# Identity products in TensorE's gaps: a planner thread that issues matrix products nobody reads

## The chip, the cores and the metric

One core of one Trainium2 chip. The metric is the device time of one execution in microseconds, lower is better. TensorE is called PE in the profile, VectorE DVE, ScalarE ACT, GpSimd POOL; SP is the engine that issues most DMAs.

## The reference, cut to what matters

Two transformer blocks, one after the other, on one sequence of 256 tokens with 1024 features in float32. Each has an adaptive modulation computed from a vector `c`, a mixer and a gated feed-forward layer of width 2816.

```python
# first block: attention and mLSTM side by side
merged = sigmoid(g_a) * (y_a @ w_branch_attn) + sigmoid(g_m) * (y_m @ w_branch_mlstm)
x = x + gate_m * rms_norm(merged @ w_out, g_post_mix)
h2 = modulate(rms_norm(x, g_pre_ffn), shift_f, scale_f)
ff = (silu(h2 @ w_ffn_gate) * (h2 @ w_ffn_up)) @ w_ffn_down
x = x + gate_f * rms_norm(ff, g_post_ffn)
# second block: gMLP and RWKV-7 side by side
x = layer_norm(x, emb_ln_g, emb_ln_b)
p = (x * (1 + sc1) + sh1) @ w_in
mix = concat([gmlp(p[..., :2*MIX_A]), rwkv7(p[..., 2*MIX_A:])]) @ w_out_2
x = layer_norm(ALPHA * x + gt1 * mix)
f = (silu(gu[..., :FFN]) * gu[..., FFN:]) @ w_ffn_out      # gu = (x * (1+sc2) + sh2) @ w_ffn_in
x = layer_norm(ALPHA * x + gt2 * f)
```

## The kernel before, in words

All large products use float32 operands split in two (`hi` and `lo` parts in a reduced type): a product is three passes, hi by hi, lo by hi, hi by lo. A weight arrives by a DMA of 512 KB into a `raw` buffer, ACT rounds it to `whi`, DVE subtracts to `wlo`, and then PE uses it. `xhi`, `xlo` and `wx` are the same thing in other buffers.

The first mixer is written out in program order, and the framework below the kernel orders its instructions. It does not have to keep program order between instructions that don't depend on each other: where the kernel wants an early one held back it says so (`issue_after` in `main`).

From the output projection of the first mixer on, a planner orders the work (`planned`, L1259, and class `Plan`). It keeps a clock of its own, a cost for each instruction (`cost`, L279) and a set of threads, which are generators that issue instructions and yield. What `Plan` emits keeps its emission order on PE, DVE, ACT and POOL. The order is fixed when the kernel is built: the chip knows nothing of the planner's clock, and an instruction without a dependency starts as soon as its engine reaches it.

Threads have ranks. Chains that follow each other step by step (norms, residuals, the RWKV recurrences) have ranks 0 to 8. The stream of weights and their products has rank 9 (`FILL`); a modulation product on PE, `ada` (L1097), has rank 10 where it is used. `turn` (L128) first steps any ready thread of rank below 9. Then it takes the ready thread of the lowest rank from 9 on, `th`. If PE is idle in the plan and `low` holds, `th` is stepped at once and what it issues has rank -1 (`boost`), ahead of all else that waits for PE:

```python
        low = idle and (self.tick(self.now) or self.warm(self.now) < WARM)
        if th and th.pe == 0 and low:
            self.step(th, True)
            return True
```

Only after that does `choose` (L152) give each engine the ready instruction of lowest rank. `warm` (L169) sums the columns of the products that ended in the last `TICK` (3.4133 us) of the planner's clock, and `WARM` is 4800 columns. A full float32 product of 128 x 128 counts 4 x 128 = 512 columns and is planned at 0.2153 us; a small product of the recurrences, in a part of the array, counts far fewer for its time.

The stream is not ready while it waits for an event ("f1.0": the first half of the next layer's input; "ya", "base0", "yb0", "yb1": results of the second mixer) or has 24 products waiting (`AHEAD`). The planned stages are: `mix1` (down projection, 215 to 237 us), `f1` and `ffn1` (to 438), `m2` (second mixer, to about 605), `mix2` (to 626), `f2` and `ffn2` (to 821), and the last norm.

PSUM tiles: `mm` has 4 buffers, `sm` 3 (`pssm`, L441), `ad` 1. The planner tracks which of them are free (`tile`, `ready`, `release`). `drop` marks a tile as no longer needed.

Of the kernel before, what the change touches and what calls it, by code (L numbers as in the profile page):

```python
# [18 lines left out]
P = 128  # L19
# [32 lines left out]
WARM = 4800.0  # L52
# [336 lines left out]
class Builder:  # L389
# [436 lines left out]
    def stream(self, jobs):  # L826
# [17 lines left out]
        while queue or nxt[0]:  # L844
# [8 lines left out]
            for y in emit(sl):  # L853
                fill()
                yield y

    @staticmethod
    def cut(sl, k, cols):

        o = k * cols % 512  # L860
        return [t[:, o:o + cols] for t in sl[0][k * cols // 512]]
# [397 lines left out]
    def planned(self, mT, close):  # L1259

        nc, io, tc = self.nc, self.io, self.tc
        fl = self.plan = Pool.plan = Plan()
        self.nc = TimedCore(fl, nc)
        self.hT, self.hid, self.acc, self.gb = {"m1": mT}, {}, {}, {}
        w1, w2 = io["w_ada"][0], io["w_ada_2"][0]
        cv1, cv2 = self.cv
        c2 = self.c2
        self.free = ["w", "w", "w"]
        self.set_phase("m1", "t2", "t2", "t2")
        fl.at["gate.mix1"] = fl.at["aff.f1"] = 0.0  # L1270
        fl.add(9, self.stream(self.weights()))

        def out(name):
            def get():
                if name not in self.hT:
                    self.hT[name] = self.new_hT(name)
                return self.hT[name]
            return get
        for b in range(NB):
            fl.add(0, self.chain_rms("mix1", b, out("f1"), "f1"), "mix1.%d0" % b)  # L1280
        fl.run("mix1.end")
        close()
        fl.drop(*mT)
        with tc.tile_pool(name="ffn1", bufs=1) as pool:
            self.open_ffn(pool, "f1")
            jobs = self.ada_gate(w1, cv1, 5, io["b_ada"], "ffn1", io["g_post_ffn"][0])
            jobs += self.ada_affine(w2, cv2, 0, c2["b1"][:, 0:8], 1, c2["b1"][:, 8:16], c2["emb_g"], c2["emb_b"], "m2")
            fl.add(8, self.ada(jobs))
            fl.add(7, self.rows2(io["emb_ln_g_2"], io["emb_ln_b_2"], "emb"), "gate.ffn1")
            fl.add(7, self.mixer2_consts(), "gate.ffn1")  # L1290
            for b in range(NB):
                fl.add(0, self.chain_ln("ffn1", b, self.rms_residual, out("m2"), "m2", lambda: self.gb["emb"]), "ffn1.%d0" % b)
            fl.add(10, self.ada(self.ada_affine(w2, cv2, 3, c2["b2"][:, 0:8], 4, c2["b2"][:, 8:16], c2["ln1_g"],
                                               c2["ln1_b"], "f2"), True), "ffn1.00")
            fl.run("ffn1.end")
            fl.drop(*self.hT["f1"])
        with tc.tile_pool(name="mix2", bufs=1) as pool:
            self.ph = Pool(pool, h=32, PP=1)
            self.hT["y2"] = None
            self.set_phase("m2", "hT")  # L1300
            self.mixer2()
            for b in range(NB):
                fl.add(0, self.chain_ln("mix2", b, self.alpha_residual, out("f2"), "f2", lambda: self.gb["ln1"]), "mix2.%d0" % b)
            fl.run("mix2.end")
            fl.drop(*self.hT["y2"])
        with tc.tile_pool(name="ffn2", bufs=1) as pool:
            self.open_ffn(pool, "f2")
            fl.add(8, self.gate(w2, cv2, 5, io["b_ada_2"], "ffn2"), "f2.x")
            fl.add(7, self.rows2(io["ln2_g_2"][0], io["ln2_b_2"][0], "ln2"), "f2.x")
            for b in range(NB):  # L1310
                fl.add(0, self.chain_ln("ffn2", b, self.alpha_residual, None, "out", lambda: self.gb["ln2"]), "ffn2.%d0" % b)
            fl.run("out.1")
# [1118 lines left out]
```

## Time and profile before

| | |
|---|---|
| median of 3 runs | 835.97 us (831.27 to 840.24) |
| the profiled execution | 835.19 us |
| its span, first to last instruction | 833.4 us |
| PE busy | 779.9 us, 94% |
| DVE busy | 582.2 us, 70% |
| ACT busy | 380.2 us, 46% |
| mean granted PE clock | 0.978 |

Rows below are from the profiled execution. A time in a row counts from the span's start. In rows of a timeline the first number is the start, the second the duration to the last end, then engine, line, operation, written tile <- read tiles, shapes and count; in brackets stands how long the engine had been idle and who released it. Line 376 is the planner's own call, so all planned instructions have it. The granted clock 1.00 is 2.4 GHz and 0.50 is 1.2 GHz; values between are means over a stretch that has both.

### The profile page before, as it was taken

The page shows a single profiled execution, that of the slowest core. Times are in us where ns is not written, and L with a number is a line of the kernel's source. Part 1 is how long each engine was busy: PE and PEld are TensorE (multiplying, and loading weights), DVE is VectorE, ACT ScalarE, POOL GpSimd, SP SyncE. Part 2 cuts the span into 40 slices and gives each one's busy share as a digit, 9 for nine tenths or more (in the row PEclk, how much of TensorE's full clock was granted, in tenths as well). Part 3 has the DMA queues.
Part 4 walks back from the last instruction along what each step waited for, and adds up shares of the span by engine and source line. Part 5 has one row for each costly group of instructions (what it writes and reads, how often), then busy time and mean ns, then how long its engine had stood idle before and what let it go on. Part 6 is the DMA issues. An engine that isn't in the chain of part 4 may idle for free.

```text
span 833.4 us, 14964 instructions
## 1 busy us (share of the span) xinstructions
PE 779.9 (94%) x5912; PEld 670.4 (80%) x5912; DVE 582.2 (70%) x1036; ACT 380.2 (46%) x599; POOL 61.7 (7%) x143
## 2 busy tenths in 40 slices
PE   4999899999989999999998999998896999999994
PEld 4778467999867999998885878886675899999883
DVE  3458766886778977876456467997559778666446
ACT  3346854454555444445425574443235444445330
POOL 3014010100020310000002011001001000000000
PEclk9999999999989999999999999999998999999997
DMA  9986489796759899997559617687445689766611
GB/s 268 319 265 178 168 289 275 215 254 179 246 157 316 259 308 261 306 311 242 186 162 265 177 51 182 171 250 207 149 126 164 183 256 300 213 201 216 212 52 51
DMA packets 205078, 178.94 MB, mean 215 GB/s; under 512 B 24052, under 2 KB 171712, under 8 KB 205008
## 3 DMA queue, kind: packets, MB, share of 16 engines
q1 hardware_dynamic: 201456, 168.37, 69.2%
q0 software_dynamic: 3552, 9.63, 3.6%
q8 instruction: 46, 0.75, 0.4%
q14 instruction: 24, 0.20, 0.1%
HBM read 175.06 MB, written 2.90 MB: 214 GB/s over the span
## 4 chain that ended last, share of the span: by engine, by line
PE 79%; DVE 11%; DMA 2%; ACT 2%; issue 2%; POOL 2%; SPq 1%; POOLq 0%; DVEq 0%; ACTq 0%
PE mm L376 53%; PE sm L376 5%; PE mm L434 4%; PE mm L435 4%; PE mm L436 4%; DVE x L376 2%; PE ad L554 1%; DVE wlo L376 1%; DVE wlo L427 1%; POOL hr_r L376 1%; DMA ada_raw<-in_w_ada_dram 1%; PE ad L376 1%; DMA raw<-in_w_in_dram 1%; SPq L376 1%; ACT whi L376 1%
## 5 line engine op out<-in xcount | busy, mean ns | idle before, releaser
L376 DVE TENSOR_TENSOR wlo<-raw,whi 128x1024 fp32r<-128x1024 f32 (+1 forms) x135 | 163.7, 1216 | 99.8 <-ACT whi L376 98.9
L376 ACT CAST whi<-raw 128x1024 fp32r<-128x1024 f32 (+1 forms) x135 | 140.7, 1045 | 187.5 <-PE mm L376 153.0
L376 PE MATMUL mm<-f_hi,wlo 128*128 128x256 f32 x560 | 156.7, 280 | 0.0
L376 PE MATMUL mm<-f_lo,whi 128*128 128x256 f32 x560 | 156.4, 279 | 0.0
L376 PE MATMUL mm<-f_hi,whi 128*128 128x256 f32 x560 | 156.0, 279 | 0.0
L376 PEld LDWEIGHTS mm<-f_lo,whi 128*128 128x128 f32 x560 | 105.8, 189 | 0.3 <-issue 0.2
L376 PEld LDWEIGHTS mm<-f_hi,whi 128*128 128x128 f32 x560 | 105.5, 188 | 0.6 <-issue 0.5
L376 PEld LDWEIGHTS mm<-f_hi,wlo 128*128 128x128 f32 x560 | 105.2, 188 | 0.7 <-issue 0.7
L427 DVE TENSOR_TENSOR wlo<-raw,whi 128x1024 fp32r<-128x1024 f32 x42 | 51.2, 1220 | 23.3 <-ACT whi L426 23.3
L426 ACT CAST whi<-raw 128x1024 fp32r<-128x1024 f32 x42 | 44.1, 1049 | 44.2 <-DMA raw<-in_w_in_dram 19.9
L434 PE MATMUL mm<-h_hi,whi 128*128 128x256 f32 (+1 forms) x184 | 52.9, 287 | 0.8 <-ACT qkv L1383 0.8
L436 PE MATMUL mm<-h_hi,wlo 128*128 128x256 f32 (+1 forms) x184 | 51.6, 280 | 0.0
L435 PE MATMUL mm<-h_lo,whi 128*128 128x256 f32 (+1 forms) x184 | 51.5, 280 | 0.0
L376 PE MATMUL mm<-m_hi,wlo 128*128 128x256 f32 (+1 forms) x152 | 42.8, 287 | 0.2
L376 PE MATMUL mm<-m_hi,whi 128*128 128x256 f32 (+1 forms) x152 | 42.4, 283 | 0.3 <-DVE kT L376 0.3
L376 PE MATMUL mm<-m_lo,whi 128*128 128x256 f32 (+1 forms) x152 | 42.3, 281 | 0.0
L434 PEld LDWEIGHTS mm<-h_hi,whi 128*128 128x128 f32 (+1 forms) x184 | 34.3, 187 | 3.1 <-ACT qkv L1383 1.7
L435 PEld LDWEIGHTS mm<-h_lo,whi 128*128 128x128 f32 (+1 forms) x184 | 34.2, 186 | 0.5 <-issue 0.5
L436 PEld LDWEIGHTS mm<-h_hi,wlo 128*128 128x128 f32 (+1 forms) x184 | 34.3, 187 | 0.0
L376 DVE SCALAR_TENSOR_TENSOR part<-ada_raw,cs,part 128x512 f32<-128x512 f32 x42 | 31.4, 746 | 0.6
L376 PE MATMUL mm<-wlo,hid_hi 128*128 128x512 f32 x80 | 31.3, 391 | 0.0
L376 PE MATMUL mm<-whi,hid_hi 128*128 128x512 f32 x80 | 31.2, 390 | 0.0
(546 smaller groups left out, 1775.3 us busy)
## 6 DMA issues: line engine op xcount, KB each, us to landing
ada_raw<-in_w_ada_dram SPq DMA_DIRECT2D x96, 512.0 KB, 5.9
raw<-in_w_in_dram SPq DMA_DIRECT2D x60, 512.0 KB, 5.5
raw<-in_w_ffn_in_dram SPq DMA_DIRECT2D x44, 512.0 KB, 5.1
raw<-in_w_ffn_gate_dram SPq DMA_DIRECT2D x22, 512.0 KB, 5.8
raw<-in_w_ffn_up_dram SPq DMA_DIRECT2D x22, 512.0 KB, 5.9
raw<-in_w_ffn_down_dram SPq DMA_DIRECT2D x22, 512.0 KB, 5.1
raw<-in_w_ffn_out_dram SPq DMA_DIRECT2D x22, 512.0 KB, 3.6
raw<-in_w_out_dram SPq DMA_DIRECT2D x16, 512.0 KB, 4.2
```

What stands on the lines that cost most here:

```text
L376: return lambda *args, **kw: self.plan.issue(self.name, op, args, kw, lambda: f(*args, **kw))
L426: self.nc.scalar.copy(hi, raw)
L427: self.nc.vector.tensor_tensor(lo, raw, hi.bitcast(F32), op=ALU.subtract)
L434: mm(out, lhsT=l[0], rhs=r[0], start=start, stop=False)
L435: mm(out, lhsT=l[0], rhs=r[1], start=False, stop=False)
L436: mm(out, lhsT=l[1], rhs=r[0], start=False, stop=stop)
L554: nc.tensor.matmul(ps[32 * g:32 * g + 32, :], lhsT=cv["rep"][:, 2 * (s - 1) + g, :], rhs=raws[s - 1 + g // 2][:, g % 2, :], start=s == 1, ...
```

## The change

A new thread of rank 30 is added when the planned part begins, and lives until the event "out.1", the end of the kernel. Whenever it is stepped while PE is free in the plan and `warm` is under `WARM`, it takes an `sm` tile, issues two float32 products of the identity with itself into its first 128 columns, drops the tile and yields until both have ended in the plan; otherwise it asks again 0.2 us later. Nothing reads the tile.

```diff
+    def keep_warm(self, until):
+
+        fl = self.plan
+        while until not in fl.at:
+            if fl.free["tensor"] <= fl.now and fl.warm(fl.now) < WARM:
+                ps = self.pssm("warm")
+                for _ in range(2):
+                    self.nc.tensor.matmul(ps[:, 0:P], lhsT=self.ident, rhs=self.ident, start=True, stop=True)
+                fl.drop(ps)
+                yield
+            else:
+                yield 0.2
+
...
         fl.add(9, self.stream(self.weights()))
+        fl.add(30, self.keep_warm("out.1"))
```

## Rows read from the trace of the kernel before

**Rows 1.** Page: granted PE clock in 40 slices of 20.8 us, in tenths.

```profile
PEclk9999999999989999999999999999998999999997
```

**Rows 2.** Stretches of 20 us: length, busy PE, PEld, DVE, ACT, POOL, then clock, DMA.

```profile
240.00:260.00 20.00, 16.65 (x62) 12.19 (x63) 17.79 (x34) 11.65 (x23) 4.02 (x6) 0.83 0.82 260
...
440.00:460.00 20.00, 16.96 (x111) 11.55 (x103) 13.27 (x25) 9.57 (x17) 3.65 (x4) 0.91 0.99 281
...
620.00:640.00 20.00, 14.28 (x62) 11.58 (x61) 18.88 (x37) 10.43 (x20) 2.43 (x4) 0.83 0.49 144
```

**Rows 3.** Stretches of 4 us, same columns, after the first and second gap.

```profile
244.00:248.00 4.00, 3.84 (x12) 2.64 (x11) 3.54 (x8) 0.00 (x0) 2.31 (x3) 0.52 0.56 177
...
448.00:452.00 4.00, 3.38 (x16) 2.41 (x20) 2.57 (x7) 1.90 (x5) 1.23 (x2) 0.66 1.14 326
```

**Rows 4.** Timeline of PE, 237 to 252 us: the first gap.

```profile
237.55 1.09 PE L376 MATMUL sm<-ident,xn 128*128 128x128 f32 x8
242.05 0.79 PE L376 MATMUL mm<-whi,f_hi 128*128 128x512 f32 x1 [3.40 <-ACT f_hi L376]
...
247.26 1.36 PE L376 MATMUL sm<-ident,xn 128*128 128x128 f32 x8 [0.16 <-DVE xn L376]
...
252.06 0.50 PE L376 MATMUL mm<-xlo,f_hi 128*128 128x512 f32 x1 [0.31 <-DVE xlo L376]
```

**Rows 5.** Stretches cut at the stages' own bounds, columns as in rows 2.

```profile
215.00:237.00 22.00, 22.00 (x97) 17.75 (x96) 15.21 (x25) 11.38 (x22) 1.51 (x3) 1.00 0.61 194
...
242.00:252.00 10.00, 8.71 (x27) 5.69 (x27) 8.43 (x19) 5.20 (x13) 2.93 (x4) 0.71 0.70 216
556.00:573.00 17.00, 13.93 (x246) 10.61 (x244) 16.34 (x43) 6.64 (x12) 1.80 (x3) 1.00 0.76 214
573.00:600.00 27.00, 24.57 (x393) 17.66 (x393) 16.08 (x33) 8.99 (x18) 2.73 (x3) 1.00 0.62 199
...
621.00:642.00 21.00, 14.66 (x62) 11.26 (x61) 20.36 (x40) 11.14 (x20) 2.43 (x4) 0.84 0.51 148
821.50:833.40 11.90, 0.06 (x1) 0.00 (x0) 7.68 (x15) 0.00 (x0) 0.54 (x1) 0.64 0.18 66
```

**Rows 6.** Timeline of PE in `m2`: full float32 products and what starts after them.

```profile
572.27 0.71 PE L376 MATMUL mm<-wsT,vv 128*128 128x128 f32 x4 [1.42 <-DVE vv L376]
573.07 0.45 PE L376 MATMUL sm<-G,M 64*64 64x64 f32 x8
...
585.69 1.16 PE L376 MATMUL mm<-wsT,vv 128*128 128x128 f32 x8
586.78 0.62 PE L376 MATMUL ad<-ada_raw,cs 128*32 128x256 f32 x2
```

**Rows 7.** Groups of PE by form, 556 to 600 us: count, busy, mean ns, idle before.

```profile
L376 PE MATMUL ad<-ada_raw,cs 128*32 128x256 f32 x80 | 6.8, 389 | 0.0
...
L376 PE MATMUL mm<-wsT,vv 128*128 128x128 f32 x16 | 2.8, 300 | 1.4 <-DVE vv L376 1.4
L376 PE MATMUL sm<-RB,W 128*64 128x64 f32 x64 | 2.8, 227 | 0.9 <-DVE F L376 0.9
```

**Rows 8.** Chain that ended last, shares by line: 572 to 604, 621 to 643, 0 to 14 us.

```profile
by line: PE sm L376 48.6%; PE mm L376 12.2%; PE ad L376 7.1%; PE adr L376 6.9%; POOL hr_r L376 5.2%; issue 4.1%; DVE gl_t L376 4.0%; DVE y L376 2.2%; DVE mix L376 2.2%; ACT rx L376 2.0%; ACT Pm L376 1.9%; ACT part L376 1.9%; ACT XT L376 1.2
...
by line: DVE x L376 24.3%; DVE wlo L376 15.4%; DVE res L376 11.2%; DVE ln_st L376 10.9%; DVE hf L376 10.6%; DVE f_lo L376 8.8%; PE mm L376 8.7%; issue 6.8%; DVE xlo L376 3.1%; DVE ln_mv L376 1.1%; DVE ln_ve L376 0.6%; DVEq L376 0.1%
...
by line: DMA ada_raw<-in_w_ada_dram 59.8%; PE sm L742 9.0%; PE ad L752 7.7%; SPq L512 5.2%; issue 3.3%; SPq L749 3.1%; SPq L629 2.5%; POOL ident L616 2.1%; POOL ident L615 1.5%; POOL vrows L510 1.1%; POOL mhalf L619 0.3%; POOLq L2420 0.1%
```

**Rows 9.** Timeline where the planned part begins, and one early POOL instruction.

```profile
10.20 1.12 POOL L1328 MEMSET invf<- 128x1 f32 x32
...
209.67 1.05 ACT L376 CAST whi<-raw 128x1024 fp32r<-128x1024 f32 x1 [1.46 <-issue]
...
215.16 0.86 PE L376 MATMUL mm<-whi,merged_hi 128*128 128x512 f32 x3
...
218.68 0.42 ACT L1672 ACTIVATE merged_hi<-mg 128x256 fp32r<-128x256 f32 x1 [1.30 <-DVE mg L1671]
```

## The prediction

> **What bounds the kernel now.** The page first: PE is busy for 94% of the span, and its granted clock has two dips ahead of the last slice [rows 1]; a third, shallower, shows only in shorter stretches. I cut the planned part into stretches of 20 us. Three of them are below full clock: 0.83, 0.91 and 0.83 [rows 2]. They are the three hand-overs from one layer to the next, where PE waits for a norm. Between them, in the big layers, PE is the bound and at 2.4 GHz: 215 to 237 us has 22.00 busy of 22.00 at clock 1.00 [rows 5].
>
> So there are two questions: what the lost clock costs on the path that sets the end, and what the new products cost where they land.
>
> The first hand-over shows how to answer the first. PE does the transposes for the first half of the tokens at 237.55, then stands for 3.40 us until ACT has made `f_hi`, and resumes at 242.05 [rows 4]. From 244 to 248 the clock is 0.52, which is 1.2 GHz nearly throughout [rows 3]; over 242 to 252 the mean is 0.71, so 2.9 us of full clock are missing [rows 5]. But PE then waits again: the next transposes (247.26) for DVE's `xn`, the product at 252.06 for DVE's `xlo` [rows 4]. What PE lost, it mostly lost inside a wait.
>
> The third hand-over is clearer. Of the chain between 621 and 643 us PE has 8.7%, nearly all of the rest are DVE's links, and DVE is busy 20.36 of 21.00 us [rows 8, 5].
>
> **The change part by part.** It removes nothing. It adds pairs of identity products wherever the planner, by its own clock, finds PE idle, fewer than 4800 columns in its look-back and no ready stream or `ada` thread. On the chip a pair has no input to wait for, so it runs as soon as PE reaches it: it is free where the next real product would have waited anyway, and costs its full time where not.
>
> *Price of a pair.* No identity product is in the trace. The nearest is `wsT` by `vv`, also full float32, 128 x 128; the trace keeps two records per product. Eight records start at 585.69 and the next product at 586.78 [rows 6]: 1.09 us for four products, 0.545 us for a pair. Bounds: four records from 572.27 to 573.07, 0.80 us a pair [rows 6]; eight transposes in 1.09 us, one record each, so 0.27 us for two [rows 4]. I take 0.545, the like operation in a run of its kind. The plan reckons 0.43.
>
> *Start of the planned part.* At the planner's time 0 its look-back is empty, and the first weight needs its DMA, ACT and DVE steps. Five pairs fill 4800 columns; they drop out again before the first product can go, so I count about 10 pairs, 5.45 us. On the chip PE has no gap there: the first planned product starts at 215.16 right behind the first mixer's last, its weight rounded at 209.67 [rows 9]. But must the pairs run there? The ACT rounding at 209.67 belongs to the plan and runs ahead of ACT's `merged_hi` at 218.68, which the program has earlier; and the rotary table's memsets (L1328) run at 10.20, in the middle of the start-up that the program has before them [rows 9]. So instructions with nothing to wait for move forward. The pairs need only the identity and an `sm` tile, and could go where PE stands still early on; there the chain is 59.8% a DMA's [rows 8]. I take 0; bounds 0 and +5.45. A gain I exclude, since that DMA doesn't end sooner.
>
> *First hand-over.* About 1.4 us after PE's last product the look-back falls below 4800, and some five pairs follow (2.7 us), inside the 3.40 us wait. The clock should stay up. Of that the path keeps the transposes alone: 1.36 us at the low clock, 1.09 at the high one [rows 4], -0.3 us. Bounds: -2.9 (all the missing clock of 242 to 252) and +0.5 (one pair in the way).
>
> *Second and third.* In the second PE is held by transposes that the plan put ahead of other work, in the belief that their input would be ready sooner. The plan sees no gap there, so I expect no pairs and 0. Bounds 0 and -1.4 (4 us at 0.66 [rows 3]). In the third some eight pairs go in front of and between the transposes, and the clock stays up, but DVE sets the pace: 0. Bounds -3.4 (20 us at 0.83 [rows 2]) and +1.1 (two pairs in the way).
>
> A rule of the Trainium skill speaks for more. "TensorE: Matmul & The Clock Gate", section "HAM oscillation — how this bites in real kernels", reckons the extra time as the throttled time times (1 - 1.2/2.4), as though every late product made the end late. Here that is 3.4 + 1.8 + 3.4 = 8.6 us, and the time would be 827.4. The waits behind the slow products [rows 4] and DVE's links [rows 8] speak against it.
>
> *Second mixer.* This is where the change costs. Between 556 and 600 us the stream waits for events, and PE does small products at clock 1.00 [rows 5]: there is no clock to win back. Small products count few columns. By the plan's formula the largest groups are `ada` (80 records, 40 products of 307), `wsT` (8 of 512) and `RB` by `W` (32 of about 118) [rows 7]; with the smaller ones, some 42,000 columns in these 44 us, where 4800 per 3.4133 us would be 61,900. The missing 19,600 are 19 pairs, nine before 573 and ten after when I count in slices of 4 us. Moreover a pair has rank -1 and is issued before `choose` looks at PE's queue: a recurrence product ready at that moment stands behind it. Nineteen pairs are 10.4 us. Before 573, 4.9 us of pairs meet 17.00 - 13.93 = 3.1 us of idle PE; the 1.8 left meet a DVE busy 16.34 of 17.00 [rows 5], and I take 0.7. After 573, 5.45 us meet 27.00 - 24.57 = 2.43 us of idle PE, and the chain is three quarters PE's (48.6 + 12.2 + 7.1 + 6.9%) [rows 8]: 3.0. Together +3.7. Bounds: 0 (all in waits) and +10.4 (none).
>
> *Tail.* PE has 0.06 us of work in the last 11.9; DVE ends the kernel [rows 5]. A dozen pairs there: 0.
>
> *Tiles.* A pair holds one of three `sm` tiles only while it runs. A recurrence product that waits for a tile can lose the turn, at the price of the pair, which the bound above contains.
>
> Sum: 0 - 0.3 + 0 + 3.7 + 0 = +3.4 us. On the profiled execution's 835.19 that is 838.6; it stands 0.78 under the median of 835.97, so the forecast is **839.4 us**.
>
> **Rivals.**
> *All the clock comes back.* Pairs hide in waits and the missing clock of the three stretches, 20 us x (0.17 + 0.09 + 0.17) [rows 2], was all on the path: -8.6, 827.4 us. For it: the pairs' place in the gaps. Against: rows 4 and 8, as said. The skill's rule above gives the same.
> *The pairs stay at the start of the plan.* About 10 pairs run between the first mixer and 215.16, where PE is without a gap: +5.45, 844.9 us. It decides if the framework holds PE's planned instructions behind the first mixer's. For it: there PE's planned products did come last [rows 9], though the data they need explain that too. Against: the early ACT and POOL instructions.
> *Priority before the recurrences.* All 19 pairs land on the chain of 556 to 600: +10.4 instead of +3.7, 846.1 us. For it: rank -1. Against: 5.5 us of idle PE.
> *Nothing.* The pairs fit the waits and the clock was not on the path, or PE's order comes out such that both cancel: 836 us.
>
> **How the numbers follow.** Forecast 0.42, its own range 837 to 843; pairs at the start 0.22; priority 0.10; nothing 0.16; all the clock 0.10. One per cent is 8.4 us (827.6 and 844.3), and about what this kernel's runs, 831.27 to 840.24, can tell from no change. Slower by over 1%: the priority case, two thirds of the start case, and 0.03 of the forecast's upper end, 0.28. Faster: the clock case at its end, 0.08, with a little for a luckier order of the recurrences, 0.10. The same: 0.62. The range 830 to 848 leaves out the clock case and the ends of the slow ones.
>
> **What would show it.** Right: `warm` products in the 237 to 242 and 626 to 635 us gaps and a clock of 1.00 in the stretches that had 0.83, without the layers behind starting sooner by more than 1 us; some 19 pairs between 556 and 605 at about 0.55 us, and that stage 3 to 4 us longer; pairs of the plan's start in the first mixer or before. Wrong: pairs in a row directly before `merged_hi`; a stage `f1` or `f2` that starts 3 us sooner; a second mixer no longer than before, or shorter, because the pairs changed the planner's choices and with them the whole order.

## The result, and the profile after

| | before | after |
|---|---|---|
| median of 6 runs | 834.85 us (831.27 to 840.24) | 848.94 us (847.08 to 852.17) |
| ratio, 95% interval | | 1.0151, 1.0115 to 1.0187 |
| the profiled execution, its span | 835.19, 833.4 us | 852.17, 850.4 us |
| PE busy | 779.9 us, 94% | 823.5 us, 97% |
| mean granted clock, profiled | 0.978 | 0.988 (0.994 to 0.996 in the other five) |

Slower by 1.5%: 12.6 us by the ratio, 14.1 by the medians, where 3.4 had been forecast. The clock did what the change wants; the time did not follow. Here and below, ratios leave out three runs (two of the kernel before, one of e9, an experiment below) that were over 1.5% longer than the fastest of their kernel.

Page of after: busy time by engine, the granted clock in 40 slices of 21 us (beside [rows 1]), and the group of the new products.

```profile
PE 823.5 (97%) x6296; PEld 716.6 (84%) x6296; DVE 583.4 (69%) x1036; ACT 381.5 (45%) x599; POOL 61.5 (7%) x143
...
PEclk9999899999999999999999999969999999999999
...
L376 PE MATMUL warm<-ident 128*128 128x128 f32 x384 | 53.5, 284 | 0.6
```

384 records are 96 pairs (two records a product, two products a pair), 53.5 us of PE, 0.557 us a pair. The dips of [rows 1] at the hand-overs and at the end are gone; one is left in the fifth slice (85 to 106 us), ahead of all pairs, and a new one stands in the 27th (553 to 574). The new one belongs to this execution, the longest of the six: the other five lack it, going by their mean clock.

Stretches of after: length, busy PE, PEld, DVE, ACT, POOL, clock, DMA, GB/s. They answer to [rows 2].

```profile
240.00:260.00 20.00, 19.02 (x108) 15.71 (x107) 17.61 (x34) 11.58 (x24) 4.03 (x6) 1.00 0.82 251
440.00:460.00 20.00, 18.07 (x152) 13.47 (x149) 12.81 (x28) 9.59 (x19) 4.05 (x6) 1.00 0.89 265
640.00:660.00 20.00, 18.18 (x108) 14.86 (x107) 19.99 (x38) 11.19 (x21) 2.44 (x4) 1.00 0.52 153
```

0.83, 0.91 and 0.83 have become 1.00 three times. Now PE's timeline of after where pairs run in blocks, beside [rows 9], [rows 4] and the last of [rows 5].

```profile
211.47 4.18 PE L376 MATMUL warm<-ident 128*128 128x128 f32 x36
215.40 1.18 PE L376 MATMUL mm<-whi,merged_hi 128*128 128x512 f32 x4
...
239.67 5.03 PE L376 MATMUL warm<-ident 128*128 128x128 f32 x32
244.45 0.48 PE L376 MATMUL mm<-whi,f_hi 128*128 128x512 f32 x1
...
836.89 12.22 PE L376 MATMUL warm<-ident 128*128 128x128 f32 x108
```

Nine pairs stand straight ahead of the first `merged_hi` product, eight fill the whole first gap, and 27 at the end run to 849.1 us, when DVE, whose work ends the kernel otherwise, has been done since 845.6 (its last row is `844.17 1.42`). PE, not DVE, now ends it, and the last stage is 1.5 us longer.

Where the 17.0 us between the two profiled spans arise, by the starts of products in the trace:

| stretch | before | after |
|---|---|---|
| to the first merged product | 215.2 | 215.4 (the first mixer's last product at 211.35) |
| `mix1`, first hand-over, to the first product with `f_hi` on the left | 56.1 | 57.8 |
| `f1`, to the first product with `hid_hi` | 105.8 | 105.8 |
| `ffn1`, second hand-over, to the first product with `m_hi` on the left | 84.4 | 86.2 |
| second mixer, `mix2`, to the last output product | 164.0 | 175.5 |
| third hand-over and `f2`, `ffn2` | 195.2 | 195.5 |
| tail | 12.7 | 14.2 |

Two thirds lie in the second mixer, but half of that belongs to this execution alone. e3 (below) has the same order and the same pairs there; in its profile the stretch has no low clock and is 5.6 us shorter, 5.9 longer than before:

```profile
464.40:634.30 169.90, 165.43 (x1697) 138.93 (x1697) 116.10 (x262) 72.60 (x130) 12.94 (x15) 1.00 0.56 158
```

The two stretches with the first two hand-overs are each 1.7 to 1.8 us longer too, although their clock is now 1.00.

### The profile page after: what moved, and what is told of

Its sections match the earlier page's. It is cut to its first block, busy times and chain, and to the rows that moved or that the text cites. A ratio compares the mean times of both kernels' runs of the same rounds, so it can differ in the third digit from the quotient of the medians.

```text
span 850.4 us, 15749 instructions
## 1 busy us (share of the span) xinstructions
PE 823.5 (97%) x6296; PEld 716.6 (84%) x6296; DVE 583.4 (69%) x1036; ACT 381.5 (45%) x599; POOL 61.5 (7%) x143
## 4 chain that ended last, share of the span: by engine, by line
PE 87%; DVE 4%; DMA 3%; ACT 2%; issue 2%; POOL 1%; SPq 1%; ACTq 0%; DVEq 0%; POOLq 0%
PE mm L376 54%; PE sm L376 7%; PE mm L434 5%; PE warm L376 4%; PE mm L435 4%; PE mm L436 4%; DMA ada_raw<-in_w_ada_dram 2%; PE ad L376 2%; PE ad L554 1%; DMA raw<-in_w_in_dram 1%; POOL hr_r L376 1%; DVE wlo L427 1%; DVE x L376 1%; PE adr L376 1%; DMA base<-image 1%
## 5 line engine op out<-in xcount | busy, mean ns | idle before, releaser
L426 ACT CAST whi<-raw 128x1024 fp32r<-128x1024 f32 x42 | 44.1, 1050 | 43.8 <-DMA raw<-in_w_in_dram 18.4
L376 PE MATMUL warm<-ident 128*128 128x128 f32 x384 | 53.5, 284 | 0.6
L376 PEld LDWEIGHTS warm<-ident 128*128 128x128 f32 x384 | 47.5, 193 | 6.5 <-issue 2.5
L376 PE MATMUL mm<-m_lo,whi 128*128 128x256 f32 (+1 forms) x152 | 44.7, 296 | 0.1
```

Of the source, the lines that this page charges most:

```text
L376: return lambda *args, **kw: self.plan.issue(self.name, op, args, kw, lambda: f(*args, **kw))
L426: self.nc.scalar.copy(hi, raw)
```

## The experiments

Each kernel ran 6 to 12 times beside the kernel before on the same chip. Every run has a span and a mean granted clock. I split each span in two: span times clock ("at full clock") and the rest ("missing", what the stretches at 1.2 GHz lacked). A pair's time, or a longer wait, shows in the first part, a lower clock in the second. The split is of totals: it doesn't say where in the kernel either arose, and a wait of the same length moves from the second part to the first when the clock rises in it. Medians over the runs:

| kernel | pairs run | planned order | ratio (95%) | at full clock | missing |
|---|---|---|---|---|---|
| before (29 runs) | 0 | before's | 1 | 816.6 | 18.4 |
| after | 96 | after's | 1.0151 (1.0115 to 1.0187) | 842.2 | 4.2 |
| e1 | 0 | after's | 1.0128 (1.0086 to 1.0169) | 816.3 | 27.9 |
| e2 | 85 | after's but one product | 1.0150 (1.0105 to 1.0195) | 839.6 | 7.6 |
| e3 | 69 | after's | 1.0137 (1.0096 to 1.0178) | 838.5 | 7.2 |
| e4 | 70 | third | 1.0146 (1.0104 to 1.0189) | 833.9 | 13.6 |
| e5 | 65 | before's | 1.0197 (1.0164 to 1.0230) | 844.9 | 4.2 |
| e6 | 0 | fourth | 1.0162 (1.0116 to 1.0207) | 820.1 | 25.8 |
| e7 | 0 | fifth | 1.0054 (1.0028 to 1.0080) | 816.4 | 23.1 |
| e8 | 0 | sixth | 1.0041 (1.0014 to 1.0068) | 816.6 | 22.2 |
| e9 | 9 | before's | 1.0031 (1.0002 to 1.0059) | 819.0 | 21.0 |
| e10 | 28 | before's | 1.0166 (1.0138 to 1.0195) | 833.6 | 15.3 |
| e11 | 12 | before's | 0.9990 (0.9968 to 1.0013) | 820.4 | 13.8 |
| e12 | 6 | before's | 0.9955 (0.9932 to 0.9979) | 814.7 | 16.2 |

The ratio is to the runs of before beside the kernel itself. The row of before is the set beside e9 to e12; the sets beside e1 to e4 (11 runs) and e5 to e8 (23 runs) give 816.3 + 17.5 and 816.7 + 19.1.

The order of instructions is fixed when a kernel is built, so it could be compared without a run: of 3826 planned products of PE, 564 stand elsewhere in after than in before.

### e1: the pairs booked, not issued

```diff
-                    self.nc.tensor.matmul(ps[:, 0:P], lhsT=self.ident, rhs=self.ident, start=True, stop=True)
+                    fl.issue("tensor", "matmul", (ps[:, 0:P],), dict(lhsT=self.ident, rhs=self.ident), lambda: None)
```

> The planner books every pair as before, but no product of it is issued, so all other instructions stand in the order of the changed kernel. If the pairs' own time on PE is what costs (theory A), this falls back to the kernel before: 835 us, or up to 838 with the low clock after the gaps back. If the new order of the second mixer is what costs (theory B), the start (4.7 us) and the end (1.5 us) come back but not the second mixer: about 843 us.

846.63 us (844.0 to 852.32): nearly all of the loss, without a single pair on the chip. At full clock it needs what before needs, 816.3; it lacks 10.4 us more of clock (27.9 against the 17.5 of its own set of before). Page of e1, the clock in 40 slices (beside [rows 1]): slices 27 and 28 (549 to 591 us), in the second mixer, are a new dip.

```profile
PEclk9999999999999999999999999978998999999997
```

Stretch of e1 there, columns as above:

```profile
557.00:597.40 40.40, 37.45 (x514) 30.94 (x513) 25.42 (x61) 12.04 (x22) 4.56 (x5) 0.80 0.55 161
```

and of before:

```profile
557.10:595.10 38.00, 32.70 (x510) 23.36 (x508) 29.12 (x65) 15.18 (x30) 4.53 (x6) 1.00 0.74 227
```

About as many products (514 and 510 records, in part other ones) occupy PE 4.75 us longer, at 0.80 against 1.00. So after's order alone costs. By the totals it costs by way of the clock, but the places don't bear that out. Here are the stretch with `mix1` and the first hand-over, then the second mixer with `mix2`, both of e1, and the first of them in before (before's second is shown at e5):

```profile
216.40:276.10 59.70, 51.65 (x217) 40.40 (x216) 45.85 (x77) 30.19 (x55) 5.69 (x9) 0.94 0.72 226
467.00:636.20 169.20, 159.86 (x1609) 133.83 (x1608) 116.06 (x262) 72.61 (x130) 12.93 (x15) 0.95 0.57 158
```

```profile
215.20:271.30 56.10, 51.40 (x216) 39.57 (x215) 44.90 (x76) 30.05 (x55) 5.68 (x9) 0.94 0.77 240
```

The second mixer lacks 8.5 us of clock and is only 5.2 us longer. The first hand-over is 3.6 us longer at the same clock, 0.94: PE stands still there for 8.05 us against 4.70, once for 2.62 us until ACT has made `xhi` (0.78 in before, at 251.24). So the new order costs by waits as well, and how much of the loss the clock makes is not shown. Against e1, after has the same order and 96 pairs more: they bring back 23.7 us of clock and add 25.9 us at full clock. The difference of the two medians, 2.3 us, is within the intervals.

### e2, e3, e4: the pairs of one place taken out

```diff
-        fl.add(30, self.keep_warm("out.1"))
+        fl.add(30, self.keep_warm("out.1"), "mix1.00")    # e2: none at the start
+        fl.add(30, self.keep_warm("ffn2.end"))            # e3: none in the tail
```

```diff
         while until not in fl.at:
-            if fl.free["tensor"] <= fl.now and fl.warm(fl.now) < WARM:
+            if "m2.1" in fl.at and "mix2.00" not in fl.at:
+                yield "mix2.00"                           # e4: none in the second mixer
+            elif fl.free["tensor"] <= fl.now and fl.warm(fl.now) < WARM:
```

> The thread begins with the event mix1.00, so the 11 pairs ahead of that are gone (9 in a row at 211 us and 2 more); the order of everything else stays but for one product. Theory A (they stand on PE's path): 849 - 4.7 = 844 us. Rival (they only fill a wait that would be there anyway, or the first mixer ends later without them): 849 us, no change.

> The thread ends with the last down product, so the 27 pairs behind it are gone; the order of everything else stays. If PE's row of pairs, 12.2 us long, outlasts DVE's last norm and the output, as the profile shows it (PE to 849.1 us, DVE to 845.6): 1.5 us less, 847.4 us. If the output transfer ends the kernel anyway: 849 us.

> No pairs between the event m2.1 and mix2.00, so 26 of 28 pairs of the second mixer are gone and the planner orders that stage without them (239 of 3826 products of PE still stand elsewhere than in the kernel before, 564 in the changed one). Theory A and theory B both say the second mixer falls back, by 9 to 11 us: 838 to 840 us. Rival: the stage is slow because it starts later or cold, or because of what the earlier pairs did to the order: 846 us or more.

848.71 us (845.42 to 853.78), 848.12 (844.22 to 849.7) and 849.13 (845.25 to 853.05): none differs from after by more than the intervals allow. In e3's profile the tail is 12.8 us again, against 12.7 before and 14.2 in after, which shows that the pairs there cost some 1.4 us; the total can't show so little. e2 is inconclusive for the same reason (see e9). e4 was meant to take away the largest part, and didn't: its order is yet another one (239 products away from before's), it is without the pairs that held the clock, and the second mixer's stretch from 558.8 to 606.9 had 0.86.

```profile
558.80:606.90 48.10, 41.30 (x581) 30.52 (x580) 32.54 (x73) 14.49 (x27) 4.78 (x6) 0.86 0.63 196
```

Taking a part out of the planner's list also changes the order, so this kind of experiment can't say what a pair costs. The next one can.

### e5, e10, e11, e9: pairs on the chip, order as before

In e5 the thread issues its pairs past the planner, on the engine itself, and keeps its own account of them. All planned operations of all engines stand exactly as in before.

```diff
+            own = [o for o in own if o[0] > fl.now - TICK]
...
-            if fl.free["tensor"] <= fl.now and fl.warm(fl.now) < WARM:
-                ps = self.pssm("warm")
+            if fl.free["tensor"] <= fl.now and fl.warm(fl.now) + sum(n for _, n in own) < WARM and fl.now >= busy and places and min(places) <= fl.now:
+                ps = self.ps.pool.tile([P, 512], F32, tag="sm", name="warm", bufs=3)
                 for _ in range(2):
-                    self.nc.tensor.matmul(ps[:, 0:P], lhsT=self.ident, rhs=self.ident, start=True, stop=True)
+                    self.nc.nc.tensor.matmul(ps[:, 0:P], lhsT=self.ident, rhs=self.ident, start=True, stop=True)
-                fl.drop(ps)
-                yield
-            else:
-                yield 0.2
+                busy = fl.now + 0.43
+                own.append((busy, 1024))
+            yield 0.2
```

> Here the pairs are really issued on TensorE, but the planner books neither their time nor their columns, so all 3826 planned products and every operation of the other engines stand in exactly the order of the kernel before; 65 pairs go in (9 to 10 ahead of the first mixer, some 30 in the second, 15 at the end). Theory, that the loss is the changed order: 836 to 839 us, ratio at most 1.004, the whole of it a possible 1.5 us at the end. Rival, that the loss is the pairs' own time on TensorE: 65 pairs of 0.55 us are 36 us, of which the share that after lost (13 of 96 x 0.55 = 53) makes some 9 us, 845 us.

851.36 us (850.04 to 854.42). My theory by then, that only the order costs, fell: with the order untouched, 65 pairs cost as much as the whole change. They bring back 14.9 us of clock and add 28.2 (against 816.7 + 19.1, their own set of before). Page of e5, the clock; then the stretch of the second mixer and `mix2` as in the table above: e5, the pairs alone in it (PE, PEld), and before.

```profile
PEclk9999999999999999999999999999999999999999
```

```profile
459.90:642.20 182.30, 174.79 (x1722) 142.82 (x1721) 115.26 (x262) 71.97 (x130) 13.25 (x15) 1.00 0.52 147
...
459.90:642.20 182.30, 19.65 (x112) 14.77 (x112) 1.00 0.52 147
```

```profile
461.50:625.50 164.00, 154.34 (x1610) 127.02 (x1610) 115.03 (x262) 71.96 (x130) 13.25 (x15) 1.00 0.59 163
```

The clock is 1.00 in both. 28 pairs (112 records) keep PE busy for 19.65 us, 0.70 us each; the stretch is 18.3 us longer, and PE's idle time in it falls only from 9.66 to 7.51. Nine tenths of the pairs' time is paid. Since PE's idle time did not grow, waits for one of the three `sm` tiles, which the pairs also use, are no large part of it.

e10 has these 28 pairs alone (`fl.add(30, self.keep_warm("mix2.00"), "m2.1")` on e5's thread):

> The order before, with 28 pairs issued but not booked, all between the last feed-forward product ahead of the second mixer and the mixer's output products. Theory, that in this stretch nearly the whole price of a pair is paid, since TensorE is busy there 94% of the time and its pauses are shorter than a pair: 28 x 0.70 us = 19.6, less the 2 us of pauses that the run with 65 unbooked pairs filled: +15 to +18 us, 851 to 855. Rival, that the second mixer's pauses hide most of them and the loss of that run sat elsewhere: 838 to 842.

850.28 us (848.08 to 854.67), +13.9 us by the ratio: most of what e5 lost, 17.0 us more at full clock against 3.1 won. Why nothing hides is in PE's timeline of e10:

```profile
563.47 0.34 PE L376 MATMUL sm<-W,RB 128*64 128x64 f32 x4
564.01 0.71 PE L866 MATMUL warm<-ident 128*128 128x128 f32 x4 [0.20 <-ACT W L376]
564.65 0.45 PE L376 MATMUL sm<-W,RB 128*64 128x64 f32 x8
565.03 0.71 PE L866 MATMUL warm<-ident 128*128 128x128 f32 x4
565.67 0.56 PE L376 MATMUL sm<-W,RB 128*64 128x64 f32 x10
566.16 0.71 PE L866 MATMUL warm<-ident 128*128 128x128 f32 x4
566.81 0.33 PE L376 MATMUL sm<-W,RB 128*64 128x64 f32 x2
```

In before this is one run, and its pause is in front:

```profile
564.24 0.93 PE L376 MATMUL sm<-W,RB 128*64 128x64 f32 x24 [0.47 <-ACT W L376]
```

The planner's clock had pauses between these products; on the chip all 24 records are ready at once. A pair that stands between them delays the next product by 0.64 us (564.01 to 564.65). In before's timeline of 557 to 600 us PE has eight pauses, 0.20 to 1.42 us, 5.3 us in all, and only two of e10's pairs in that stage have a pause in front of them.

e11 has only the pairs of the first two hand-overs (`fl.add(30, self.keep_warm("m2.1"))` on e5's thread):

> The order before, with twelve pairs issued but not booked, nine in the first hand-over and three in the second, none in the second mixer or at the end. Theory, that the clock held there gives nothing back, since the weight stream (DMA share 0.9 to 1.05 in the stretch behind) sets the pace: 835 to 838 us. Rival, that the granted clock rises from 0.84 to 1.00 in the first hand-over and the time follows: 832 to 834.

835.98 us (832.32 to 840.87): no difference. Stretch of e11:

```profile
230.00:252.00 22.00, 18.67 (x100) 14.48 (x99) 18.27 (x38) 14.15 (x31) 5.68 (x9) 1.00 0.56 179
```

and of before:

```profile
230.00:252.00 22.00, 17.35 (x68) 12.40 (x67) 17.23 (x38) 13.32 (x32) 5.68 (x9) 0.84 0.53 164
```

The clock goes from 0.84 to 1.00, and the time from the first `f_hi` product to the first with `f_hi` on the left from 29.3 to 30.3 us. The timelines show what became of the clock. Products of e11, whose first `f_hi` product starts at 239.55 (242.05 in before):

```profile
244.85 1.06 PE L376 MATMUL sm<-ident,xn 128*128 128x128 f32 x8 [1.48 <-DVE xn L376]
...
248.53 0.50 PE L376 MATMUL mm<-xhi,f_hi 128*128 128x512 f32 x1 [0.78 <-ACT xhi L376]
...
250.61 1.50 PE L866 MATMUL warm<-ident 128*128 128x128 f32 x12
251.87 0.48 PE L376 MATMUL mm<-whi,f_hi 128*128 128x512 f32 x1
```

and of before:

```profile
251.24 0.50 PE L376 MATMUL mm<-xhi,f_hi 128*128 128x512 f32 x1 [0.78 <-ACT xhi L376]
...
253.33 0.39 PE L376 MATMUL mm<-whi,f_hi 128*128 128x512 f32 x1
```

From the first `f_hi` product to the first with `xhi` before needs 9.19 us at the low clock and e11 8.98 at the high one: 0.2 us won. The rest became waiting, most of it the 1.48 us ahead of the transposes where before waits 0.16 us [rows 4]. They wait for DVE's `xn`, which itself waits for POOL's `rms_r`: the norm of the other half of the tokens sets the pace, and not the weight stream that the expectation named. Behind it three more pairs stand where PE has no pause, and the next product comes 1.26 us late. Nothing gives that back: from there to the first product with `f_hi` on the left e11 needs 17.93 us and before 17.98. So the 1.0 us is pairs paid for, not waiting.

e9 has the nine pairs of the start alone, issued by hand where after has them (`for _ in range(9)`, two products each, ahead of `fl.add(30, ...)`, without the thread):

> The kernel before with nine pairs and nothing else: issued on TensorE straight behind the last product of the first mixer and ahead of the first merged product, the place of the 4.18 us block of after; every other instruction stands as before. Theory A, that TensorE sets the end there: the block's 4 us show in full, 839 to 841 us against 836.5 (ratio 1.003 to 1.006). Theory B, that the weight stream sets the pace and gives the block back: 835.5 to 837.5.

840.61 us (834.26 to 847.16), 0.3% longer by the ratio, 2.6 us, and barely apart from nothing: its interval begins at 1.0002. Its stretch, whole and of the pairs alone, shows the block unhidden, 4.18 us in 15.00 in which PE never pauses:

```profile
205.00:220.00 15.00, 15.00 (x119) 14.49 (x119) 11.46 (x20) 8.59 (x14) 0.00 (x0) 1.00 0.67 201
...
205.00:220.00 15.00, 4.18 (x36) 4.10 (x36) 1.00 0.67 201
```

### e6, e7, e8: the planner disturbed, nothing issued

e6 books four pairs after the first mixer's output has begun, e8 one pair behind the last `ffn1` product; e7 books no time, only the columns.

```diff
+                n += 1                                   # e6: 4, from "mix1.00"; e8: 1, from "m2.1"
+                if n == 4:
+                    return
```

```diff
+            if fl.free["tensor"] <= fl.now and fl.warm(fl.now) < WARM and fl.now >= busy:   # e7
+                busy = fl.now + 0.43
+                fl.columns += 1024
+                fl.busy.append((busy, 1024))
+            yield 0.2
```

> Nothing is issued for the pairs; the planner books four of them (0.43 us each, 1.7 us in all) after the first mixer has begun and none after that. 565 of 3826 planned products then stand elsewhere than in the kernel before, about as many as in after (564). Theory, that the order before was a good draw and almost any disturbance of the planner ends in a worse one: 841 to 848 us. Rival, that the loss comes from the many pairs booked in the second mixer, which keep the planner from pulling weight products forward there: 836 us, as before.

> No pair is issued and none takes time in the plan; only the planner's count of recent columns is raised as a pair would raise it, so that it less often gives weight products priority over ready ones. 153 planned products stand elsewhere than before, all after the first mixer. If the count alone (priority no longer given) makes the loss: 843 to 847 us, the second mixer and its residual 5 to 11 us longer. If the time booked makes it: 835 to 838 us.

> The planner books one pair, 0.43 us, at the first idle moment of TensorE after the last feed-forward product ahead of the second mixer; nothing is issued. 105 planned products move, all from there on. If any disturbance of the second mixer's order costs: 839 to 845 us. If it takes many pairs: 835 to 837 us.

849.25 us (843.45 to 855.32), 839.92 (838.35 to 843.66), 839.13 (834.79 to 844.95). Four bookings of 0.43 us, none of them in the second mixer, move 565 products and cost 1.6%; one moves 105 and costs 0.4%. Columns alone cost 0.5%. So the loss of e1 needs neither many pairs nor pairs in the second mixer. e7 fell between its two expectations, e6 above the one it bears out. In the table most of the loss is again missing clock, against their own set of before: 6.7 of e6's 10.1 us there, all of e7's and e8's. The places again don't follow it: e6's profile has 4.9 us of missing clock in the second mixer and `mix2`, and yet the stretch is 1.2 us shorter than before's 164.0:

```profile
476.30:639.10 162.80, 153.73 (x1571) 129.51 (x1570) 115.37 (x261) 72.00 (x129) 14.00 (x15) 0.97 0.55 151
```

That the order before is simply a good one among many fits all four disturbed orders with no pair on the chip (e1, e6, e7, e8), each slower; four are too few to call it shown. Which products' places cost the time was not tried.

### e12: pairs where the trace shows a long pause

```diff
+            if b == 1:
+                pw = self.pssm("warm")
+                for _ in range(12):
+                    nc.tensor.matmul(pw[:, 0:P], lhsT=self.ident, rhs=self.ident, start=True, stop=True)
             mx = self.sm([P, 8], "att_mx")
```

This is the kernel before with six pairs in the first mixer's attention, in the one place of that mixer with a pause longer than 3 us in front of products and 1.2 GHz behind it. (The first hand-over, with 3.40 us [rows 4], is another such place in the kernel; e11 is the experiment on it.)

> The kernel before with six pairs in the one place where its trace shows TensorE idle for over 3 us: the first mixer at 97.6 to 101.15 us, where the adaptive-norm products wait for VectorE and the 4 us behind run at 1.2 GHz. The pairs are issued behind the second block's score products. Theory, that pairs pay where the idle time is longer than they are and TensorE sets the pace behind it: 2 to 4 us faster, 832.5 to 834.5. Rival, that DMA sets the pace there too (its share is over 1 from 106 us on): 836 to 837; or the order of the first mixer, which shifts by some ten instructions, costs more than it gives: above 838.

832.25 us (830.38 to 840.66), 0.45% faster than before (0.21 to 0.68%). Timeline of PE in before, then in e12:

```profile
97.00 0.62 PE L434 MATMUL mm<-whi,h_hi 128*128 128x512 f32 x2
101.15 3.54 PE L554 MATMUL ad<-ada_raw,cols 128*32 128x512 f32 x10 [3.53 <-issue]
```

```profile
91.66 1.14 PE L1408 MATMUL sm<-kT,qT 64*128 64x256 f32 x8
92.73 2.94 PE L1417 MATMUL warm<-ident 128*128 128x128 f32 x24
95.43 0.48 PE L436 MATMUL mm<-whi,h_lo 128*128 128x512 f32 x1
...
99.06 1.88 PE L554 MATMUL ad<-ada_raw,cols 128*32 128x512 f32 x10 [0.84 <-issue]
```

and 8 us from just behind the pause's begin, in before and, at the same place of its work, 2.09 us earlier, in e12:

```profile
98.00:106.00 8.00, 4.85 (x16) 1.75 (x17) 7.94 (x18) 6.59 (x21) 0.00 (x0) 0.79 0.23 60
```

```profile
95.91:103.91 8.00, 7.16 (x33) 4.48 (x33) 7.90 (x20) 6.35 (x21) 0.11 (x1) 1.00 0.33 102
```

In before the modulation products start 7.40 us after the score products (93.75 to 101.15), in e12 too (91.66 to 99.06): the block moves the weight products behind it into the pause and delays nothing that counts. Then the products run at 2.4 GHz, the ten modulation records in 1.88 us instead of 3.54, 33 records where there were 16, and the DMAs start again sooner (102 GB/s against 60). Both parts of the sum fall, 1.9 and 2.2 us.

That accounts for 1.7 us. The 2.09 us by which e12's profile leads lie ahead of the pairs, so they are not theirs. Nor does the clock fall behind this pause in every execution: over the other thirteen profiles, all without pairs there, the ten records take 1.88 to 3.59 us. The shortest is e4's:

```profile
99.30 1.88 PE L554 MATMUL ad<-ada_raw,cols 128*32 128x512 f32 x10 [3.53 <-issue]
```

So the pairs explain up to 1.7 us of the 3.8. Some ten instructions of the first mixer change places too, and no run has that order without the pairs; whose the rest is stays open.

## Why the prediction was right or wrong

Slower was right, the size not: 839.4, within 1% of before, was forecast; 848.94 came, 1.5% slower and 0.9 us above the top of the range. Two steps failed: the second mixer's +3.7 was too small for the pairs' own time, and the changed order of all other instructions was put at nothing.

*Price of a pair: right as a mean, wrong where it counted.* 0.545 forecast; 0.557 over all. But blocks run at 0.46 (4.18 us for nine) and lone pairs at 0.70. The upper bound, 0.80, was the nearer row for the second mixer.

*Second mixer: the term that was mis-sized.* "Together +3.7" let pairs meet PE's idle time: 4.9 us against 3.1, 5.45 against 2.43. e5 shows the step false: of 19.65 us of pairs 2.2 went into idle time. The planner's pauses aren't the chip's, so comparing totals of idle time with totals of pairs says nothing of their meeting. The rival "priority before the recurrences" had the right size, +10.4 for 19 pairs; e10's 28 cost 13.9, and 0.50 each is 9.4 for 19. Its reason, rank -1, is not what e10 shows: there no pair passed through the planner's queue. They are late because they stand in order between ready products. The count of 19 was for 556 to 605; after has 14 pairs (56 records) there and 22 (88) between 465 and 641 us.

*The whole order: left out of the sum.* It stood in the last paragraph as a sign of being wrong ("the pairs changed the planner's choices"), without a price or a chance. On its own it makes nearly the whole loss: e1, 10.7 us by its ratio, with no pair at all. The plan books each pair, and everything after it is chosen at another time; that could be read from `account`, and one booking (e8) moves 105 products.

*Start of the planned part: wrong place.* The step "instructions with nothing to wait for move forward" failed for these pairs; they stand where the rival put them, nine in 4.18 us ahead of `merged_hi`. Alone they cost 2.6 us (e9), within the bounds 0 and +5.45.

*Hand-overs: right that the clock comes back and the time doesn't; wrong on the pairs.* In e11 the clock of the first hand-over won 0.2 us up to the `xhi` product, where 0.3 was forecast. But some five pairs inside the 3.40 us wait were forecast, and after has eight: ACT has `f_hi` under way at 242.51, 1.13 us later than before, and the first `f_hi` product starts at 244.45, 2.40 later, so the pairs delay it by 1.3 us. In the second no pairs were expected, and after has nine (36 records, 5.04 us, between 443 and 465). The third, with `f2`, takes 135.3 us against 135.0, as forecast.

The Trainium skill's rule ("TensorE: Matmul & The Clock Gate", section "HAM oscillation — how this bites in real kernels") reckons throttled time times (1 - 1.2/2.4) as extra time. It doesn't hold at the hand-overs: e11 won 4.6 us by that reckoning and at most 0.3% of time. Nor does it hold by place in e1, whose second mixer lacks 8.5 us and is 5.2 longer.

*Tail: wrong by 1.4 us.* "A dozen pairs there: 0" holds for e5's fifteen (6.86 us, tail 12.8); after has 27, and they outlast DVE.

*The sum.* The effects don't add up in one column: after's order costs about 10.7 us by itself, in the totals nearly all of it missing clock; its pairs give the clock back (23.7) and cost 25.9. What in the new order costs the 10.7 us stays open.

## What to carry to other kernels

Filler work is free only in a pause of the chip, so its place is read from a trace and not from a scheduler's clock: with six pairs in one measured pause the kernel was 0.45% faster (1.7 us of that seen at the pause), and 28 in pauses that only the planner saw lost 1.7%. A scheduler that books filler chooses differently from there on; separate the two effects by booking without issuing and by issuing without booking before either is believed. Clock won in a stretch that another engine paces comes back as waiting. Splitting each run's span into full-clock time and missing clock shows what was traded for what over all runs, but not where: set the stretches of the traces beside it before a loss is put down to the clock.

## What the runs showed of the hardware that was not expected

The same order of instructions meets the low clock in some executions and not in others. e9 and e11 have before's order in the second mixer and no pairs there, and yet ran 14.4 us at a mean of 0.70 and 0.66 where before has 1.00. e9, e11, then before:

```profile
597.90:612.30 14.40, 14.40 (x146) 11.42 (x145) 3.29 (x9) 2.24 (x4) 0.00 (x0) 0.70 0.01 1
...
594.70:609.10 14.40, 14.40 (x148) 11.37 (x144) 3.46 (x10) 1.63 (x3) 0.00 (x0) 0.66 0.00 1
...
597.10:611.50 14.40, 13.38 (x136) 10.53 (x132) 4.82 (x11) 3.72 (x5) 1.67 (x1) 1.00 0.13 38
```

Their whole stretches to the last output product took 169.7, 170.8 and 164.0 us. A second such place is the first mixer: in before PE stands still for 1.27 us ahead of `adc<-sel,part` (at 133.94, waiting for ACT's `part`), and the clock is 0.50 from 136 to 138; in after PE has no pause there and in e8 one of 0.53 us, and the clock stays at 1.00. From a product just ahead of the pause (131.00 in before) to the first with `h_hi` on the left behind it (140.46) before needs 9.46 us, after 6.31 and e8 7.10: 2.4 to 3.1 us for the pause and what follows. A third is the pause of e12, at which the clock fell behind the same 3.53 us in some profiles and not in e4's.

That these places make the spread of before's own runs (831.26 to 841.20 us among those the ratios use) is not shown, since only one of them has a trace. It fits the runs: over the 61 of the three sets, all of one order, the mean granted clock goes from 0.969 to 0.985, and by a straight line through each set a run that lacks 1 us more of clock is 0.65 to 0.89 us longer. One profiled execution of each kernel could not have told a change of 5 us in either of the first two places from chance; the medians could.
